# A step's preparation split into two streams, with three expected times set anew, in a planned recurrent layer

## The chip, the cores and the metric

The kernel runs on one core of one Trainium2 chip. The metric is the device time of one execution in microseconds, the median of three runs. TensorE (PE) multiplies, VectorE (DVE) and ScalarE (ACT) do elementwise work and empty PSUM, GpSimd (POOL) helps, and SyncE (SP) issues the DMAs.

## The reference

One layer over 1024 prompt tokens and 8 x 16 sample tokens, model width 1024, 16 heads of 64. In short form:

```python
h = rmsnorm(x, g_norm); proj = h @ w_in            # columns: r k v w_lr a_lr z_a | gb gc xb z_b | g_a g_b
pa = proj_a + mu_shift * (previous_token - proj_a)   # token shift on r, k, v, w_lr, a_lr, z_a
w = exp(-c * sigmoid(w_decay0 + tanh(w_lr) @ w_decay2)); a = sigmoid(w_iclr0 + a_lr @ w_iclr2)
kt = k * (1 + (a - 1) * k_replace); kh = k * k_removal / norm_of_head(k * k_removal)
# for each token: S = S * w - (S kh) (a * kh)^T + v kt^T ;  y = S r
o_a = (group_norm(y) + sum_of_head(r * kt * r_bonus) * v) * silu(z_a)
out_b = (gb * conv3(gc * xb) * silu(z_b)) @ w_o_b
x = x + (sigmoid(g_a) * (o_a @ w_o_a) + sigmoid(g_b) * out_b) @ w_out
x = x + sigmoid(rmsnorm(x, g_ple) @ w_ple_gate) * (p @ w_ple); y = rmsnorm(x, g_final)
```

It also returns the new states. The recurrence is computed in chunks of 64 tokens.

## The kernel before, in words

Every projection is a "dense": 8 steps over the contraction, of three f16 matmuls each (high and low parts), into one of two PSUM banks of the pool `psd`. Tokens come in three blocks: 512 prompt tokens, the 128 sample tokens, 512 prompt tokens. Heads come in 8 pairs. A *step* is one pair and one block, so there are 24 steps; step `i` has pair `j = i // 3` and block `g = i % 3`.

Most of the time is one loop (`go`), in which the order of TensorE's instructions is planned when the program is built. Ten kinds of work are Python generators; a `Stream` runs one kind, one step (or column tile) at a time. The planner keeps a clock of its own, `pe[0]`, which each matmul advances by a cost. A generator yields a number (not before so many us from now), a number and a count of PSUM banks of the pool `psp` that it needs, a condition, or DENSE or MORE (a part of a projection comes next). `go` first takes a stream that isn't a projection and is due, in the order of the list `every`; if there is none it takes a projection part, one begun before a new one. Convolution projections (`conv`) go ahead of the others when they are behind a pace counted in chunks of the recurrence, and behind them otherwise. The order that comes out is TensorE's order on the chip; the other engines' orders are made by the scheduler from the order of the program and priorities.

The streams of a step:

- `prep` (L365): `decay` multiplies the low-rank inputs (`lod`, `loa`) and makes the decay products `pb` and `pi`; then the projections `k`, `r`, `v`, `z` in this order, each mixed with the token before it (`mixed`). After `r`, squares of `k` are summed per head (`pss`, 4.0 us expected) and the inverse norms `rnb` made by a chain of small VectorE operations and one ScalarE copy (L442). Before `v`, the generator waits until the tail of step `i - 3` is through (`S_tail.at >= f.i - 2`; `v` and `zs` have three buffers). After `v`, 3.0 us expected, `rnb` is transposed (`prn`), and `k`, `kt` and `tha` are finished on VectorE. After `z` comes its tanh, then `keys`.
- `keys` (L467) makes the operands `ar` and `kb` of the scores (`kb` has one buffer: it waits for `kb_done` of the step before) and `rkt`.
- `scores` (L497) waits until the step before has read its scores (`m_done`, `x_done`), then, 1.0 us expected, multiplies `kb` and `ar` (`psc`) into two banks. `values` transposes `kb` and `v` (`pk`, `pv`). `inverse` (`itt`, `ig`, `i`, `ie`, `if`) inverts the chunks' triangular matrices. `chain` is the recurrence, three matmuls per chunk (`c`, `u`, `u`), 8 chunks in a prompt step and 2 in a sample step. `tail` makes the output (`y`, `py`).
- `opening` brings in the three blocks at the start, `conv` makes the other branch, and `gates_b` computes up to six merge gates (`EARLY`) into DRAM once the convolution is done and as long as tails are left.

Behind the loop come the remaining gates, the three output projections and the embedding stage; an early gate is loaded from DRAM (`gb_d`) there.

Ring buffers that matter: seven stage buffers (`TA`) for the intermediate tiles of `prep`, and six pairs of projection weights (`whi`, `wlo`), loaded on SP and split by ScalarE and VectorE; the weights of the next pair are loaded when the third block has used those of this pair.

Of the kernel before, what the change touches and what calls it, by code (L numbers as in the profile page):

```python
# [23 lines left out]
RN = 512  # L24
# [47 lines left out]
def _build(nc, tc, I, O, top):  # L72
# [292 lines left out]
    def prep(f):  # L365
# [39 lines left out]
            tha, pb, pt, pi = yield from decay()  # L405

        m = {}
        ahead = g == 2 and j + 1 < 8
        for q, t in (("k", T_K), ("r", T_R), ("v", T_V), ("z", T_ZA)):
            load_q(j, q)  # L410
            if q == "v":
                yield lambda: S_tail.at >= f.i - 2
            ps = yield from dense_parts(s.w[q], blk, q + nm)
            if ahead:
                load_q(j + 1, q)
            if q == "v":
                x = f.v = tt(wk, "v", "v" + nm, 3, RN)[:, :n]
            elif q == "z":
                x = f.zs = tt(wk, "zs", "zs" + nm, 3, RN)[:, :n]
            else:  # L420
                x = tt(st_, "ta", q + nm, TA)[:, :n]
            mu = (zmu[:, i, j:j + 1] for i in range(3)) if q == "z" else (
                P("mu", t + j), mum[:, t + j:t + j + 1], mus[:, t + j:t + j + 1])
            mixed(ps, t + j, blk, x, *mu, q + nm)
            m[q] = x
            if q == "k" and not f.i:
                f.k_done = True
                tha, pb, pt, pi = yield from decay()
            if q == "r":
                x = m["k"]  # L430
                yield 4.0

                sq = tt(st_, "ta", "sq" + nm, TA)[:, :n]
                A.activation(sq, x, AF.Square, scale=P("krem", j))
                pss = psa.tile([128, 512], F32, tag="a", name="pss" + nm)
                for i in range(npr):
                    mm(pss[:, 2 * i:2 * i + 2], sq[:, i * 128:(i + 1) * 128], onesb[:, 0:128:64], start=True, stop=True)
                ssm = small.tile([128, 8], F32, tag="ssm", name="ssm" + nm)
                V.tensor_scalar(out=ssm[:, :2 * npr], in0=pss[:, :2 * npr], scalar1=1e-24, scalar2=None, op0=ALU.max)
                rn = rsqrt(ssm[:, :2 * npr], 2 * npr, "k%d" % npr)  # L440
                rnb = tt(st_, "ta", "rnb" + nm, TA)[:, :n]
                A.activation(rnb.rearrange("p (q t) -> p q t", t=64), rn.unsqueeze(2).to_broadcast([128, 2 * npr, 64]),  # L442
                             AF.Copy)
            if q == "v":

                k = m["k"]
                yield 3.0
                prn = psa.tile([128, 512], F32, tag="a", name="prn" + nm)
                for i in range(npr):
                    tr(prn[:, i * 128:(i + 1) * 128], rnb[:, i * 128:(i + 1) * 128], ident)  # L450
                kt = tt(st_, "ta", "kt" + nm, TA)[:, :n]
                V.tensor_scalar(out=kt, in0=tha, scalar1=half[:, 2, j:j + 1], scalar2=half[:, 3, j:j + 1],
                                op0=ALU.mult, op1=ALU.add)
                V.tensor_tensor(out=kt, in0=kt, in1=k, op=ALU.mult)
                V.scalar_tensor_tensor(out=k, in0=k, scalar=P("krem", j), in1=prn[:, :n], op0=ALU.mult, op1=ALU.mult)
                V.scalar_tensor_tensor(out=tha, in0=tha, scalar=1.0, in1=k, op0=ALU.add, op1=ALU.mult)
        if ahead:
            load_lora(j + 1)
        z = m["z"]

        thz = tt(st_, "ta", "thz" + nm, TA)[:, :n]
        A.activation(thz, z, AF.Tanh)
        V.scalar_tensor_tensor(out=f.zs, in0=thz, scalar=1.0, in1=z, op0=ALU.add, op1=ALU.mult)
        f.pt = pt
        yield from keys(f, m["k"], kt, tha, m["r"], pb, pi)

    def keys(f, kh, kt, b2, r, pb, pi):  # L467
        j = f.j
# [28 lines left out]
    def scores(f):  # L497
# [7 lines left out]
        np2 = min(2, npr)  # L505
        msk = sm_s if smp else sm_p
        for p0 in range(0, npr, 2):
            yield 1.0, 2
            pss = [psp.tile([128, 2, 2, 128], F32, tag="p", name=f"psc{nm}_{p0}{h}")[:, :np2] for h in range(2)]
            for p in range(np2):  # L510
                for e in range(2):
                    for x in range(2):
                        for h, H in enumerate(HS):
                            mm(pss[h][HS[x], p, e, :], kb[H, p0 + p, 2 * e + x, :],
                               ar[H, 2 * (p0 + p) + e].rearrange("p a b -> p (a b)"), start=True, stop=True)
            hold(1.3)
            hold(2.2)
            for h in range(2):
                pf4 = pss[h].rearrange("p c e (x t) -> p c (e x) t", x=2)
                V.tensor_tensor(out=scx[:, h, p0:p0 + np2], in0=pf4[:, :, 1:3, :],  # L520
                                in1=msk[:, 64:128].unsqueeze(1).unsqueeze(1).to_broadcast([128, np2, 2, 64]), op=ALU.mult)
                V.tensor_tensor(out=scy[:, h, p0:p0 + np2], in0=pf4[:, :, 0:4:3, :],
                                in1=msk[:, 0:64].unsqueeze(1).unsqueeze(1).to_broadcast([128, np2, 2, 64]), op=ALU.mult)
# [348 lines left out]
    class Stream:  # L872
# [28 lines left out]
        def fill(self):  # L901
            return self.next in (DENSE, MORE)

    S_chain, S_tail, S_val, S_inv, S_scores, S_open, S_prep, S_conv, S_gate = every = [
        Stream(k) for k in (chain, tail, values, inverse, scores, opening, prep, conv, gates_b)]
    may = {S_chain: lambda i: S_inv.at > i and S_val.at > i and S_tail.at >= i - 1,
           S_tail: lambda i: S_chain.at > i,
           S_val: lambda i: S_scores.at > i and S_chain.at >= i - 1 and (i < 2 or steps[i - 2].y_done),
           S_inv: lambda i: S_scores.at > i,
           S_scores: lambda i: S_prep.at > i and (i < 3 or steps[i - 3].y_done),  # L910
           S_prep: lambda i: S_chain.at >= i - 3 and S_open.at >= (0, 2, 3)[min(i, 2)],
# [31 lines left out]
    rk.close()  # L943


    ow = top.enter_context(tc.tile_pool(name="ow", bufs=1, side="right"))
    mr = top.enter_context(tc.tile_pool(name="mr", bufs=1, side="right"))
    oo = top.enter_context(tc.tile_pool(name="oo", bufs=1))
# [45 lines left out]

    obs = []
    for j in range(KT):
        if T_GB + j not in EARLY:
            gate(ms[j], T_GB + j, f"b{j}")
            for k in range(2 * (j - 4), 2 * (j - 3)):
                obs.append(load_o(ob_d, k, f"b{k}"))  # L1000
    for j in range(KT):
        if T_GB + j in EARLY:
            SP.dma_start(ms[j], gb_d[EARLY.index(T_GB + j)])
        w = load_wr(I["w_ob"][j], f"b{j}")
        for blk in BL3:
            o, n = blk
            ps = dense_r(w, obs, blk, f"ob{j}_{o}")
            V.scalar_tensor_tensor(out=ms[j][:, o:o + n], in0=ms[j][:, o:o + n], scalar=1.0, in1=ps,
                                   op0=ALU.add, op1=ALU.mult)
# [2 lines left out]

    def gate_a(j):
        gts[j] = op.tile([128, NTOK], F32, tag="gt", name=f"gt{j}", bufs=2)
        if T_GA + j in EARLY:
            SP.dma_start(gts[j], gb_d[EARLY.index(T_GA + j)])
        else:
            gate(gts[j], T_GA + j, f"a{j}")

# [242 lines left out]
```

## Time and profile before

| what | value |
|---|---|
| median of 3 runs | 1888.74 us (1888.63 to 1889.81) |
| the profiled execution | 1887.54 us |
| its span, first to last instruction | 1885.7 us |
| TensorE busy | 1795.6 us (95%) |
| VectorE busy | 1250.5 us (66%) |
| ScalarE busy | 815.2 us (43%) |
| granted clock of TensorE, mean | 0.991 |

The profile is of one execution. Busy time counts the union of an engine's instructions; matmuls overlap, and their ends are modelled. Names are the program's tiles: `dk`, `dr`, `dv`, `dz` are the projections of a step, `dC`, `dx`, `dzb`, `dB` those of the convolution, `dgb`, `dga` the gates.

### The profile page before, as it was taken

The numbers are of one execution on the slowest core, as the hardware profiler recorded it, in microseconds if no ns is written. First come the engines' busy times: TensorE is split into PE (matmuls) and PEld (weight loads), VectorE is DVE, ScalarE is ACT, GpSimd is POOL, SyncE is SP. The second block draws the span as 40 slices with busy tenths as digits, with TensorE's granted clock in tenths as the row PEclk, the third lists the DMA queues.
The fourth block names the chain that finished last, engine by engine and source line by source line (L and its number), as shares of the span: only waits on it lengthen the run. The fifth ranks groups of instructions, "written<-read, shape, count | busy, mean of one in ns | idle before, by whom it ended". The sixth has DMA issues, their size and how long they took to land.

```text
span 1885.7 us, 37719 instructions
## 1 busy us (share of the span) xinstructions
PE 1795.6 (95%) x15326; PEld 1242.4 (66%) x15326; DVE 1250.5 (66%) x3181; ACT 815.2 (43%) x1871; POOL 210.8 (11%) x333
## 2 busy tenths in 40 slices
PE   5999999999999999999999999999999999999997
PEld 2555665565666666566566556565499777999865
DVE  5577887788688788788788878861422411545566
ACT  6454463554555446446446446442311311333332
POOL 1001121111112111111101101100000011200000
PEclk9999999999999999999999999999999999999998
DMA  6011102011111101101100200221512410242012
GB/s 223 12 35 49 53 17 76 22 33 54 36 33 48 52 31 42 60 31 36 63 31 24 76 29 16 64 86 64 170 58 65 133 45 23 85 157 91 13 32 79
DMA packets 45198, 110.65 MB, mean 59 GB/s; under 512 B 6368, under 2 KB 21344, under 8 KB 45024
## 3 DMA queue, kind: packets, MB, share of 16 engines
q1 hardware_dynamic: 45024, 108.24, 17.9%
q8 instruction: 120, 1.97, 0.4%
q14 instruction: 54, 0.44, 0.1%
HBM read 87.94 MB, written 20.28 MB: 57 GB/s over the span
## 4 chain that ended last, share of the span: by engine, by line
PE 66%; DVE 20%; ACT 7%; DMA 3%; issue 2%; POOL 1%; SPq 0%; DVEq 0%; ACTq 0%
PE ob L92 5%; PE oc L92 5%; PE oa L92 5%; PE dr L92 4%; PE pg L92 4%; PE dz L92 4%; PE dga L92 4%; PE dgb L92 4%; PE dk L92 3%; PE dB L92 3%; PE dzb L92 3%; PE dv L92 3%; PE u L92 2%; PE dC L92 2%; PE dx L92 2%
## 5 line engine op out<-in xcount | busy, mean ns | idle before, releaser
L92 PEld LDWEIGHTS <-whip 128*128 128x128 f16 x1536 | 132.7, 99 | 72.1 <-issue 6.5
L687 POOL TENSOR_SCALAR Spt<-sbd,pt 128x128 f32<-128x128 f32 x128 | 91.3, 713 | 612.0 <-DVE sbd L706 611.0
L706 DVE SCALAR_TENSOR_TENSOR sbd<-u,pt,Spt 64x64 f32<-64x64 f32 x256 | 72.1, 282 | 68.7 <-PE u L92 65.7
L92 PEld LDWEIGHTS <-wlop 128*128 128x128 f16 x768 | 75.5, 98 | 61.8 <-issue 2.2
L92 PE MATMUL dgb<-hx,whigb 128*128 128x512 f16 (+1 forms) x480 | 110.4, 326 | 3.9 <-ACT ms L993 3.5
L627 ACT ACTIVATE bdgt<-ig 64x512 f16<-64x512 f32 (+1 forms) x208 | 106.5, 512 | 2.7
L92 PE MATMUL dB<-hx,whiB 128*128 128x512 f16 (+1 forms) x384 | 90.5, 331 | 4.4 <-ACT sho L233 4.4
L92 PE MATMUL dx<-hx,whiX 128*128 128x512 f16 (+1 forms) x384 | 90.1, 328 | 2.8 <-ACT sho L240 2.8
L92 PE MATMUL dC<-hx,whiC 128*128 128x512 f16 (+1 forms) x384 | 89.9, 328 | 2.1 <-ACT sho L233 2.1
L92 PE MATMUL dzb<-hx,whiZ 128*128 128x512 f16 (+1 forms) x384 | 88.1, 326 | 3.4 <-ACT sho L233 1.7
L92 PE MATMUL dv<-hx,whip 128*128 128x512 f16 (+1 forms) x384 | 90.1, 329 | 0.9 <-DVE zb L829 0.9
L694 ACT ACTIVATE yst<-c 64x128 f32<-64x128 f32 x144 | 38.9, 270 | 119.4 <-DVE xs L693 117.6
L92 PE MATMUL dz<-hx,whip 128*128 128x512 f16 (+1 forms) x384 | 90.5, 329 | 0.0
L92 PE MATMUL dr<-hx,whip 128*128 128x512 f16 (+1 forms) x384 | 90.0, 329 | 0.0
L92 PE MATMUL dk<-hx,whip 128*128 128x512 f16 (+1 forms) x384 | 88.1, 326 | 0.0
L92 PEld LDWEIGHTS <-pg 128*128 128x128 f16 x768 | 65.7, 99 | 27.7 <-issue 3.2
L620 ACT ACTIVATE gt<-ig 128x512 f16<-128x512 f32 (+1 forms) x104 | 54.2, 521 | 67.1 <-PE ig L92 66.6
L628 DVE CAST_PREDICATED tt<-cph,i 128x512 f16<-128x512 uint16 (+1 forms) x104 | 61.8, 594 | 29.9 <-PE i L92 26.0
L700 ACT ACTIVATE vu<-u 64x64 f32<-64x64 f32 x288 | 62.7, 218 | 39.8 <-PE u L92 36.2
L92 PE MATMUL dgb<-hx,wlogb 128*128 128x512 f16 (+1 forms) x240 | 74.4, 326 | 0.0
L634 DVE CAST_PREDICATED tn<-cph,i 128x512 f16<-128x512 uint16 (+1 forms) x104 | 61.3, 589 | 9.1 <-PE i L92 8.8
L92 PEld LDWEIGHTS u<-xs,tm 128*128 128x128 f32 x288 | 51.7, 192 | 22.6 <-DVE xs L693 5.4
(332 smaller groups left out, 4898.3 us busy)
## 6 DMA issues: line engine op xcount, KB each, us to landing
wstp<-i_w_in SPq DMA_DIRECT2D x32, 512.0 KB, 3.5
wstgb<-i_w_in SPq DMA_DIRECT2D x10, 512.0 KB, 3.5
xt<-i_x SPq DMA_DIRECT2D x9, 512.0 KB, 6.1
ob_d<-zb SPq DMA_DIRECT2D x8, 576.0 KB, 2.9
ostb<-ob_d SPq DMA_DIRECT2D x24, 192.0 KB, 2.6
osta<-oa_d SPq DMA_DIRECT2D x24, 192.0 KB, 2.5
xr<-i_xT SPq DMA_DIRECT2D x8, 576.0 KB, 3.6
wstC<-i_w_in SPq DMA_DIRECT2D x8, 512.0 KB, 3.5
```

The source lines that it names most:

```text
L92: PE.matmul(out, lhsT, rhs, start=start, stop=stop)
L620: A.activation(Gt, pg, AF.Copy, scale=-1.0)
L627: A.activation(Gb[R, :, R], pg[R], AF.Copy, scale=-1.0)
L628: V.copy_predicated(out=Tt, mask=bc(lvt[:, b, :]).bitcast(U16), data=p1)
L634: V.copy_predicated(out=Tn, mask=bc(lv[:, b, :]).bitcast(U16), data=p2)
L687: G.tensor_scalar(out=Spt, in0=S, scalar1=pt[:, c:c + 1], scalar2=None, op0=ALU.mult)
L694: A.activation(yst[Vh, p, :], pc[Vh, 0:128], AF.Copy)
L700: A.activation(vu[Uh, c, H], pu[H, H], AF.Copy, scale=-1.0)
L706: V.scalar_tensor_tensor(out=S2[H, H], in0=pu[H, 128 + h * 64:192 + h * 64], scalar=pt[H, c:c + 1], in1=Spt[H, H], op0=ALU.mult, op1=ALU.add)
```

## The change

`prep` is split. A new stream, `prep_v`, makes `v` and `z` and the gate `zs`; `prep` keeps `decay`, `k`, `r`, the norms and `keys`. The steps that the four projections share become the function `project`. `prep_v` stands before `prep` in the list of streams; its step `i` may start when the tail of step `i - 3` is through, which `prep` no longer waits for, and `values` waits for it. Three numbers change: the transposed norms are expected 8.0 us after the sums (3.0 us after `v` before), the first scores of a step 5.0 us after they may start (1.0 before), and the list of gates that count as early becomes as long as the loop got.

```diff
@@ -405,24 +405,8 @@
             tha, pb, pt, pi = yield from decay()
 
         m = {}
-        ahead = g == 2 and j + 1 < 8
-        for q, t in (("k", T_K), ("r", T_R), ("v", T_V), ("z", T_ZA)):
-            load_q(j, q)
-            if q == "v":
-                yield lambda: S_tail.at >= f.i - 2
-            ps = yield from dense_parts(s.w[q], blk, q + nm)
-            if ahead:
-                load_q(j + 1, q)
-            if q == "v":
-                x = f.v = tt(wk, "v", "v" + nm, 3, RN)[:, :n]
-            elif q == "z":
-                x = f.zs = tt(wk, "zs", "zs" + nm, 3, RN)[:, :n]
-            else:
-                x = tt(st_, "ta", q + nm, TA)[:, :n]
-            mu = (zmu[:, i, j:j + 1] for i in range(3)) if q == "z" else (
-                P("mu", t + j), mum[:, t + j:t + j + 1], mus[:, t + j:t + j + 1])
-            mixed(ps, t + j, blk, x, *mu, q + nm)
-            m[q] = x
+        for q in "kr":
+            x = m[q] = yield from project(f, q)
             if q == "k" and not f.i:
                 f.k_done = True
                 tha, pb, pt, pi = yield from decay()
@@ -441,10 +425,9 @@
                 rnb = tt(st_, "ta", "rnb" + nm, TA)[:, :n]
                 A.activation(rnb.rearrange("p (q t) -> p q t", t=64), rn.unsqueeze(2).to_broadcast([128, 2 * npr, 64]),
                              AF.Copy)
-            if q == "v":
 
                 k = m["k"]
-                yield 3.0
+                yield 8.0
                 prn = psa.tile([128, 512], F32, tag="a", name="prn" + nm)
                 for i in range(npr):
                     tr(prn[:, i * 128:(i + 1) * 128], rnb[:, i * 128:(i + 1) * 128], ident)
@@ -454,15 +437,36 @@
                 V.tensor_tensor(out=kt, in0=kt, in1=k, op=ALU.mult)
                 V.scalar_tensor_tensor(out=k, in0=k, scalar=P("krem", j), in1=prn[:, :n], op0=ALU.mult, op1=ALU.mult)
                 V.scalar_tensor_tensor(out=tha, in0=tha, scalar=1.0, in1=k, op0=ALU.add, op1=ALU.mult)
-        if ahead:
+        if g == 2 and j + 1 < 8:
             load_lora(j + 1)
-        z = m["z"]
-
-        thz = tt(st_, "ta", "thz" + nm, TA)[:, :n]
+        f.pt = pt
+        yield from keys(f, m["k"], kt, tha, m["r"], pb, pi)
+
+    def project(f, q):
+
+        j, nm, blk = f.j, f.nm, f.blk
+        s = pair(j)
+        t = {"k": T_K, "r": T_R, "v": T_V, "z": T_ZA}[q]
+        load_q(j, q)
+        ps = yield from dense_parts(s.w[q], blk, q + nm)
+        if f.g == 2 and j + 1 < 8:
+            load_q(j + 1, q)
+        if q in "vz":
+            x = tt(wk, "v" if q == "v" else "zs", ("v" if q == "v" else "zs") + nm, 3, RN)[:, :blk[1]]
+        else:
+            x = tt(st_, "ta", q + nm, TA)[:, :blk[1]]
+        mu = (zmu[:, i, j:j + 1] for i in range(3)) if q == "z" else (
+            P("mu", t + j), mum[:, t + j:t + j + 1], mus[:, t + j:t + j + 1])
+        mixed(ps, t + j, blk, x, *mu, q + nm)
+        return x
+
+    def prep_v(f):
+
+        f.v = yield from project(f, "v")
+        z = f.zs = yield from project(f, "z")
+        thz = tt(st_, "ta", "thz" + f.nm, TA)[:, :f.blk[1]]
         A.activation(thz, z, AF.Tanh)
         V.scalar_tensor_tensor(out=f.zs, in0=thz, scalar=1.0, in1=z, op0=ALU.add, op1=ALU.mult)
-        f.pt = pt
-        yield from keys(f, m["k"], kt, tha, m["r"], pb, pi)
 
     def keys(f, kh, kt, b2, r, pb, pi):
         j = f.j
@@ -505,7 +509,7 @@
         np2 = min(2, npr)
         msk = sm_s if smp else sm_p
         for p0 in range(0, npr, 2):
-            yield 1.0, 2
+            yield 1.0 if p0 else 5.0, 2
             pss = [psp.tile([128, 2, 2, 128], F32, tag="p", name=f"psc{nm}_{p0}{h}")[:, :np2] for h in range(2)]
             for p in range(np2):
                 for e in range(2):
@@ -901,11 +905,12 @@
         def fill(self):
             return self.next in (DENSE, MORE)
 
-    S_chain, S_tail, S_val, S_inv, S_scores, S_open, S_prep, S_conv, S_gate = every = [
-        Stream(k) for k in (chain, tail, values, inverse, scores, opening, prep, conv, gates_b)]
+    S_chain, S_tail, S_val, S_inv, S_scores, S_open, S_pv, S_prep, S_conv, S_gate = every = [
+        Stream(k) for k in (chain, tail, values, inverse, scores, opening, prep_v, prep, conv, gates_b)]
     may = {S_chain: lambda i: S_inv.at > i and S_val.at > i and S_tail.at >= i - 1,
            S_tail: lambda i: S_chain.at > i,
-           S_val: lambda i: S_scores.at > i and S_chain.at >= i - 1 and (i < 2 or steps[i - 2].y_done),
+           S_pv: lambda i: S_tail.at >= i - 2 and S_open.at >= (1, 2, 3)[min(i, 2)],
+           S_val: lambda i: S_scores.at > i and S_pv.at > i and S_chain.at >= i - 1 and (i < 2 or steps[i - 2].y_done),
            S_inv: lambda i: S_scores.at > i,
            S_scores: lambda i: S_prep.at > i and (i < 3 or steps[i - 3].y_done),
            S_prep: lambda i: S_chain.at >= i - 3 and S_open.at >= (0, 2, 3)[min(i, 2)],
@@ -943,6 +948,8 @@
     rk.close()
 
 
+    early = EARLY[:S_gate.at]
+    assert len(early) >= 4
     ow = top.enter_context(tc.tile_pool(name="ow", bufs=1, side="right"))
     mr = top.enter_context(tc.tile_pool(name="mr", bufs=1, side="right"))
     oo = top.enter_context(tc.tile_pool(name="oo", bufs=1))
@@ -994,13 +1001,13 @@
...
-        if T_GB + j not in EARLY:
+        if T_GB + j not in early:
...
-        if T_GB + j in EARLY:
-            SP.dma_start(ms[j], gb_d[EARLY.index(T_GB + j)])
+        if T_GB + j in early:
+            SP.dma_start(ms[j], gb_d[early.index(T_GB + j)])
...
```

## Rows read from the trace of the kernel before

**Rows 1.** Busy time, share of the span and instructions of two engines, from the page

```profile
PE 1795.6 (95%) x15326; PEld 1242.4 (66%) x15326; DVE 1250.5 (66%) x3181; ACT 815.2 (43%) x1871; POOL 210.8 (11%) x333
```

**Rows 2.** Busy time by stretch: start and end, length, then each engine

```profile
core 0: us, PE busy (x) PEld busy (x) DVE busy (x) ACT busy (x) POOL busy (x), PEclk, DMA share, GB/s
0.00:97.00 97.00, 71.78 (x448) 40.58 (x448) 56.94 (x134) 56.51 (x100) 8.21 (x22) 0.95 0.34 118
...
97.00:1341.00 1244.00, 1197.59 (x11588) 756.15 (x11587) 960.34 (x2555) 616.90 (x1495) 176.13 (x287) 0.99 0.15 46
...
640.00:787.40 147.40, 142.72 (x1419) 91.26 (x1417) 121.69 (x325) 77.09 (x188) 22.02 (x37) 1.00 0.13 43
787.40:934.80 147.40, 142.63 (x1418) 91.16 (x1417) 121.62 (x325) 77.02 (x188) 22.02 (x37) 1.00 0.13 42
1215.00:1341.00 126.00, 122.66 (x1041) 73.24 (x1040) 58.05 (x151) 43.43 (x105) 9.35 (x14) 1.00 0.25 87
```

**Rows 3.** TensorE's waits, 640 to 787 us: total us, times, longest

```profile
PE c L92 <- DVE sbd L706: 0.8, 1, 0.8
PE pk L96 <- DVE scy L522: 0.8, 1, 0.8
...
PE psc L92 <- DVE scy L522: 0.5, 2, 0.3
```

**Rows 4.** TensorE's waits, 97 to 545 us

```profile
PE dB L92 <- ACT sho L233: 4.4, 2, 2.3
PE dx L92 <- ACT sho L240: 2.8, 2, 2.5
PE dC L92 <- ACT sho L233: 2.1, 1, 2.1
```

**Rows 5.** TensorE in order of time, 745 to 833 us: start, length, instruction

```profile
745.47 1.05 PE L92 MATMUL pss<-cpk,sq 128*128 128x2 f32 x8 [0.27 <-ACT vu L551]
...
756.42 0.66 PE L96 MATMUL py<-ident,yc 128*128 128x128 f32 x4 [0.34 <-DVE yc L761]
...
758.43 0.59 PE L92 MATMUL dv<-hx,whip 128*128 128x512 f16 x2 [0.23 <-DVE zb L829]
...
768.55 0.63 PE L96 MATMUL prn<-ident,rnb 128*128 128x128 f32 x4
...
778.20 1.10 PE L92 MATMUL psc<-ar,kb 64*64 64x128 f32 x32
...
809.89 1.03 PE L92 MATMUL pss<-cpk,sq 128*128 128x2 f32 x8
...
815.01 0.45 PE L92 MATMUL y<-vu,scy 128*64 128x64 f32 x8
...
829.86 0.40 PE L92 MATMUL if<-tn,bdgt 128*128 128x64 f16 x8
...
832.69 0.38 PE L92 MATMUL c<-sbd,ar 128*128 128x128 f32 x2
```

**Rows 6.** Busy time in three stretches behind waits and one unbroken gate projection

```profile
316.00:319.30 3.30, 3.30 (x10) 1.29 (x9) 0.00 (x0) 0.00 (x0) 0.00 (x0) 0.50 0.33 130
469.60:472.90 3.30, 3.30 (x12) 2.01 (x11) 1.88 (x4) 0.44 (x2) 0.00 (x0) 0.50 0.17 71
111.20:114.60 3.40, 3.12 (x15) 1.49 (x15) 2.35 (x8) 0.58 (x2) 0.62 (x3) 0.50 0.01 2
1473.00:1484.30 11.30, 11.30 (x72) 5.88 (x72) 5.93 (x10) 5.56 (x11) 0.00 (x0) 1.00 0.52 160
```

**Rows 7.** ScalarE in order of time: the norms of two steps

```profile
757.35 0.63 ACT L442 ACTIVATE rnb<-nrk 128x512 f32<-128x512 f32 x1 [2.75 <-DVE nrk L139]
...
816.37 0.63 ACT L442 ACTIVATE rnb<-nrk 128x512 f32<-128x512 f32 x1 [0.85 <-DVE nrk L139]
```

**Rows 8.** VectorE in order of time: the key products of one step

```profile
762.41 0.68 DVE L489 TENSOR_TENSOR kb<-kt,pi 128x512 f32<-128x512 f32 x1
...
773.57 0.69 DVE L490 SCALAR_TENSOR_TENSOR kb<-tha,pi 128x512 f32<-128x512 f32 x1
```

More of the change, by code (lines that the diff above doesn't have):

```diff
@@ L1014, in gate_a @@
         gts[j] = op.tile([128, NTOK], F32, tag="gt", name=f"gt{j}", bufs=2)
-        if T_GA + j in EARLY:
-            SP.dma_start(gts[j], gb_d[EARLY.index(T_GA + j)])
+        if T_GA + j in early:
+            SP.dma_start(gts[j], gb_d[early.index(T_GA + j)])
         else:
```

## The prediction

> **What bounds the kernel now.** I read the page's busy shares first, then busy time by stretch, then who TensorE waited for, and last the order of events around one step of the third block. TensorE is busy 1795.6 us of a span of 1885.7, VectorE 1250.5 [rows 1]. By stretch, three regimes show [rows 2]: an opening of 97 us with 25.2 us idle, the recurrent loop from 97 to 1341 us with 46.4 us idle in 1244, and a projection stage with hardly any. Inside the loop the picture repeats every 147.4 us, the time of one pair of heads: the two stretches shown hold 142.7 and 142.6 us of TensorE work, so 4.7 and 4.8 us idle. No gap is left that one could close at one place: the steady idle is made of waits of 0.8 us and less [rows 3], while VectorE is busy 121.7 of the 147.4 us. The larger waits all lie before 545 us: projections that wait until ScalarE has emptied a PSUM bank (4.4 + 2.8 + 2.1 us) [rows 4].
>
> The chain of the recurrence does pause. In the pair shown, the short sample chain ends before 815.01 us (its `y`), and the next chain's first matmul stands at 832.69, right after that step's inverse (`if`, 829.86) [rows 5]. That inverse is late because its step is: the sums `pss` come at 745.47, but `v` only at 758.43, after `py` of an older tail at 756.42; then `prn` at 768.55 and the scores at 778.20 [rows 5]. So 17.7 us of pause per pair hang on a wait for a tail that keys don't need. But TensorE doesn't pause there; projections fill it. The reader should hold two facts apart: the chain has slack in it, TensorE has almost none.
>
> The Trainium skill (Perfetto Trace Analysis, Identifying the Most-Contended Engine) says that matmul busy time is a bad measure of distance to the roofline, and that the share of LDWEIGHTS should be used. By it the pair at 640 us (91.3 of 147.4 us, 62%) would leave room, and closing the pause would pay 17.7 us a pair. The trace disagrees: 72 projection matmuls that run without a break fill 11.30 of 11.30 us with only 5.9 us of weight loads (52%) [rows 6], so 62% is no room here.
>
> **The change part by part.** Times are set against the profiled execution, 1887.5 us (span 1885.7 and 1.8 around it); the median of the runs is 1.2 higher, so a difference is added to 1888.7.
>
> *Matmuls, DMAs, operations.* None is added or removed in the loop: the same four projections, sums, transposes and scores per step, and the same weight loads, which stay attached to the projection that they precede (the next pair's `v` and `z` weights are now issued from the value stream). Sum: 0. The list of early gates becomes as long as the loop got; a gate that isn't made in the loop is made later, 11.30 us for 72 matmuls [rows 6] at either place, and its trip through DRAM falls away. That is 0 as long as gates still cover the loop's end; the loop's last stretch is 122.7 of 126 us busy [rows 2], and the four gates behind the loop stay there as cover.
>
> *Keys no longer wait for the tail.* Scores, inverse and chain of the third block can come up to 17.7 us earlier. What hides this is TensorE's own work: 142.7 us a pair must be done anyway, and the convolution is paced by chunks, so a chain that gets ahead calls in convolution work and is slowed again. Value 0. Its bounds: nothing, or at best all idle time of the loop, 46.4 us.
>
> *Transposed norms: 3.0 us after `v` become 8.0 us after the sums.* In the step at 745.47 the norms `rnb` were ready at 757.35 + 0.63, so 12.5 us after the sums began; in the next step 7.1 us (809.89 to 816.37 + 0.63) [rows 5, 7]. Neither cost anything, because `v`'s projection lay between. Now TensorE's queue reaches `prn` 8.0 us after the sums' 0.9 us, so 8.9 us. A step like the second waits 0, one like the first 3.6 us, and behind `prn` the whole queue waits, chain matmuls too. Bounds: 0, or 3.6 in one step of each of 8 pairs, 29 us. I take 4 us, nearer to the cheap row: keys now run earlier against the tail whose VectorE work made that step late.
>
> *Scores: 1.0 becomes 5.0 us.* `z`'s projection stood between `prn` and the scores. In the step shown the last key product ended at 773.57 + 0.69, 5.7 us after `prn` began [rows 5, 8]; the allowance is now 0.5 + 5.0. So 0.2 us a step are missing. But the first key product ended at 762.41 + 0.68, 17.6 us after the sums, and `prn` now comes after 8.9; if VectorE serves it no sooner, scores at 8.9 + 5.5 wait 3.2 us. Bounds 0 and 8 x 3.2 = 26 us; I take 2, since scores also wait for the preceding step's values.
>
> *`v` and `z` back to back.* In the sample step these are short projections. PSUM has two banks for projections, and the trace shows the price of two short ones in a row: `dx` waits 2.5 us for a bank, and behind that wait the granted clock is 0.5, the 1.2 GHz level, from 111.2 to 114.6 us [rows 4, 6], which costs up to 1.7 us more. Bounds: 0, because chain and inverse matmuls between them cover it (the steady pairs show no such wait), or 4.2 us in each of 8 pairs, 34 us. I take one such event, 4 us.
>
> *Waits that dissolve.* The order of projections is drawn anew, so the three kinds of bank waits before 545 us (9.3 us) and the slow clock behind three of them (3 x 1.7) [rows 6] need not recur; steady pairs live without them. Bounds 0 and -14.4; I take -12, all but one.
>
> The wait for the tail moves to a stream on which only projections `v` and `z` are queued; `values` waits for it, and needs it only after the previous chain. 0, and covered by convolution work; if that were used up, the pause above would come back, at 17.7 us a pair.
>
> *Moved along.* The next pair's low-rank weights (four small DMAs on SP, one ScalarE and one VectorE operation) are issued ahead of `v` and `z` instead of behind; they are needed a step later, so 0. The tanh of `z` takes one of seven stage buffers that the keys also use; if none is free, ScalarE's queue stands until the norms are transposed. The nearest row is its 2.75 us of idle time before `rnb` [rows 7]; bounds 0 and 2.8 us in each of 8 pairs, 22 us. I take 0, because ScalarE is busy only 77 of 147.4 us [rows 2].
>
> At the start, `v` and `z` of step 0 now precede `r`, and its scores wait 4 us longer; other projections cover both, 0, and at most 4 us.
>
> Sum: 4 + 2 + 4 - 12 = -2 us, so **1886.7 us**.
>
> **Rivals.** *A: norms late (slower).* VectorE is busy 82% of a pair [rows 2]; if the sums of one step per pair still fall beside a tail, `prn` blocks the queue. Seven pairs at 3.6 us instead of my 4 in all: 1886.7 + 21 = 1908, and 1920 if the slow clock follows each. It decides from norms later than 8.9 us. For it speaks the 12.5 us, against it the 7.1. *B: short projections collide (slower).* 4.2 us in every other pair gives 1886.7 + 13 = 1900, in every pair 1917. *C: the loop loosens (faster).* With keys ready ahead of need, scores and inverse no longer crowd the same microseconds; the 14.4 us go and half of the steady 4.7 us in the last five pairs, 12 us: 1888.7 - 26 = 1862 at best, and half of it 1876. *D: TensorE has room (faster).* Then seven pauses close, 7 x 17.7 = 124: 1765 us. The 4.7 us of idle a pair speak against it. The page of the Trainium skill named above would have it so. *E: it doesn't do what it says.* The scores could be held by something else than their keys; then order and waits stay, 1888.7. For it speaks that scores wait for their PSUM banks, too (0.5 us a pair) [rows 3]; against it that those of the third block start 9.6 us behind `prn`, once `z` is through [rows 5].
>
> **How the numbers follow.** A measurement can tell about 0.2%, 3.8 us. My forecast, work kept and small waits traded, has 0.35, with a range of its own of 1880 to 1895: 0.13 faster, 0.18 the same, 0.04 slower. A has 0.17 and B 0.12, all slower. C has 0.20 and D 0.03, all faster. E has 0.13: 0.09 the same, 0.02 and 0.02 to either side. Sums: faster 0.38, same 0.27, slower 0.35. From 1870 to 1908 little is left out: D, the best part of C and the worst parts of A and B.
>
> **What would show it.** TensorE's loop work stays 142.7 us a pair; the waits column then decides. `prn <- rnb` at zero clears A, a row of 20 us or more proves it. `dz`, `dk` or conv projections waiting for ScalarE prove B. Scores of the third block should follow their sums by some 15 us instead of 32.7, and the pause of 17.7 us should shrink while the pair's 147.4 us do not. If the pair shortens below 143 us, my reading of TensorE as full is wrong.

## The result, and the profile after

The change makes the kernel slower: 1933.83 us (1933.39 to 1937.75, 4 runs) against 1888.68 us (4 runs of before on the same chip), a ratio of 1.0248 [1.0232, 1.0264]. The forecast was 1886.7, with a range up to 1908.

The page's busy shares and the windows of the kernel after, to be read beside [rows 1, 2]:

```profile
PE 1796.6 (93%) x15326; PEld 1244.0 (64%) x15326; DVE 1249.6 (65%) x3181; ACT 815.9 (42%) x1871; POOL 227.1 (12%) x333
```

```profile
0.00:97.00 97.00, 71.41 (x459) 40.23 (x460) 54.53 (x132) 54.61 (x99) 8.98 (x22) 0.96 0.35 120
97.00:1387.00 1290.00, 1199.08 (x11579) 758.33 (x11577) 963.54 (x2560) 620.45 (x1497) 190.58 (x287) 0.99 0.14 45
1387.00:1931.60 544.60, 526.09 (x3291) 445.43 (x3290) 231.57 (x492) 140.88 (x276) 27.56 (x24) 0.99 0.24 75
```

TensorE does the same work (1796.6 us against 1795.6), and so does the loop (1199.1 against 1197.6). The loop ends 46 us later, and its idle time is 1290 - 1199.1 = 90.9 us where it was 46.4: 44.5 us more, the whole loss. The opening and the stage behind the loop keep theirs (25.6 and 18.5 us now).

TensorE's waits in this loop, the largest rows, and two small ones on which the forecast rested (total us, times, longest):

```profile
PE py L96 <- DVE yc L765: 9.0, 5, 3.7
PE psc L92 <- DVE bdgt L651: 8.1, 3, 4.1
PE py L96 <- ACT vu L555: 5.7, 3, 2.4
PE dk L92 <- ACT sho L240: 5.6, 3, 2.6
PE dC L92 <- ACT sho L240: 5.0, 3, 2.5
PE lod L92 <- ACT vu L555: 5.0, 9, 1.5
PE dx L92 <- ACT sho L233: 4.9, 2, 3.3
PE dC L92 <- ACT cs L793: 3.4, 4, 1.5
...
PE prn L96 <- ACT rnb L426: 2.7, 2, 1.6
PE dr L92 <- ACT sho L233: 2.6, 1, 2.6
```

No row dominates; there are many waits of one to four microseconds, most of them for a PSUM bank. The largest row is not: `py` transposes `yc`, and waits until VectorE has scaled it (L765). The view that gives idle time by group of instructions allows a sum by the PSUM pool that the waiting matmul writes into:

| pool: tiles | before, 97 to 1341 us | after, 97 to 1387 us |
|---|---|---|
| `psd`: projections (`dB`, `dx`, `dzb`, `dC`, `dv`, `dk`, `dr`, `dgb`) | 4.4 + 2.8 + 3.4 + 2.1 + 0.9 + 0 + 0 + 0.4 = 14.0 | 2.3 + 6.6 + 3.9 + 8.4 + 0.4 + 10.2 + 7.2 + 0 = 39.0 |
| `psa`: small tiles (`py`, `lod`, `prn`, `psb`, `pss`, `y`) | 5.7 + 0 + 0 + 1.9 + 1.1 + 0 = 8.7 | 15.2 + 5.6 + 3.3 + 0.7 + 0.3 + 0.3 = 25.4 |
| `psp`: scores, values, inverse | 14.8 | 20.5 |
| `psc`: the chain (`c`, `u`, `pS`) | 4.9 + 3.1 + 0 = 8.0 | 1.1 + 4.3 + 0.3 = 5.7 |

So +25.0 for projections, +16.7 for small tiles, +5.7 for scores and what follows them, -2.3 for the chain; with 0.8 less before the first output projection, and rounding, that is the 44.5. Not all of it is waiting for a bank: of the small tiles' 25.4 us, 9.0 are `py` waiting for `yc` and 2.7 `prn` waiting for the norms `rnb` (5.7 and 0 before).

One of these waits in TensorE's order of time, with ScalarE beside it:

```profile
1025.59 0.38 PE L92 MATMUL lod<-lrd,lwh 128*128 128x512 f16 x1 [1.53 <-ACT vu L555]
...
1026.02 0.27 PE L92 MATMUL dv<-hx,whip 128*128 128x128 f16 x2
...
1029.76 0.28 PE L92 MATMUL dz<-hx,whip 128*128 128x128 f16 x2
...
1031.55 0.22 PE L92 MATMUL dz<-hx,wlop 128*128 128x128 f16 x1
1034.38 0.59 PE L92 MATMUL dk<-hx,whip 128*128 128x512 f16 x2 [2.61 <-ACT sho L240]
```

```profile
1032.08 0.62 ACT L397 ACTIVATE pb<-cum 128x512 f32<-128x512 f32 x1
1032.60 0.62 ACT L401 ACTIVATE pi<-cum 128x512 f32<-128x512 f32 x1
1033.23 0.37 ACT L226 ACTIVATE v<-dv,mum 128x128 f32<-128x128 f32 x1
...
1034.15 0.18 ACT L240 ACTIVATE sho<-dv 128x8 f32<-128x8 f32 x1 [0.29 <-DVE v L238]
```

`dv` and `dz` of the sample block are short and now stand back to back. `dz` is done in 2.0 us, and the next key projection needs the bank that `dv` left. ScalarE is busy with other work, the decay products `pb` and `pi` last, reads `dv` at 1033.23, 3.5 us after its last matmul began (1029.70), and the bank is free after the copy of the last tokens at 1034.15. Behind `dk` all of TensorE's queue stands for 2.61 us.

### The profile page after: what moved, and what is told of

The parts are those of the page before. It is cut to its first block, busy times and chain, and to the rows that moved or that the text cites. A ratio compares the mean times of both kernels' runs of the same rounds, so it can differ in the third digit from the quotient of the medians.

```text
span 1931.6 us, 37755 instructions
## 1 busy us (share of the span) xinstructions
PE 1796.6 (93%) x15326; PEld 1244.0 (64%) x15326; DVE 1249.6 (65%) x3181; ACT 815.9 (42%) x1871; POOL 227.1 (12%) x333
## 4 chain that ended last, share of the span: by engine, by line
PE 65%; DVE 22%; ACT 6%; issue 3%; DMA 3%; POOL 0%; POOLq 0%; SPq 0%; DVEq 0%; ACTq 0%
PE ob L92 5%; PE oc L92 5%; PE oa L92 5%; PE dgb L92 4%; PE pg L92 4%; PE dr L92 4%; PE dC L92 4%; PE dga L92 4%; PE dv L92 3%; PE dk L92 3%; PE dzb L92 3%; PE dz L92 3%; PE dx L92 3%; PE dB L92 2%; PE u L92 2%
## 5 line engine op out<-in xcount | busy, mean ns | idle before, releaser
L92 PE MATMUL dk<-hx,whip 128*128 128x512 f16 (+1 forms) x384 | 88.7, 326 | 10.2 <-ACT sho L240 5.6
L92 PE MATMUL dzb<-hx,whiZ 128*128 128x512 f16 (+1 forms) x384 | 88.8, 326 | 3.9 <-ACT sho L233 3.3
L92 PE MATMUL dz<-hx,whip 128*128 128x512 f16 (+1 forms) x384 | 89.2, 327 | 0.0
L632 DVE CAST_PREDICATED tt<-cph,i 128x512 f16<-128x512 uint16 (+1 forms) x104 | 61.8, 595 | 20.3 <-PE i L92 18.5
L697 DVE TENSOR_TENSOR xs<-c,vu 64x128 f32<-64x128 f32 x144 | 41.3, 287 | 43.7 <-PE c L92 41.2
```

The lines of the kernel that those rows point to most:

```text
L92: PE.matmul(out, lhsT, rhs, start=start, stop=stop)
L632: V.copy_predicated(out=Tt, mask=bc(lvt[:, b, :]).bitcast(U16), data=p1)
L697: V.tensor_tensor(out=xs[Uh, :], in0=pc[Uh, 0:128], in1=vu[Uh, c, :], op=ALU.add)
```

## The experiments

The view and stretch named with a number are those of the run in question; the kernel before beside each run gave 1887.7 to 1889.3 us.

**One part undone, one part alone.** First the scores: the new 5.0 taken back, and the 5.0 alone in the kernel before.

```
e1 (after):   yield 1.0 if p0 else 5.0, 2   ->  yield 1.0, 2
e2 (before):  yield 1.0, 2                  ->  yield 1.0 if p0 else 5.0, 2
```

> The changed kernel with the first scores of a step expected 1.0 us after they may start, as before, instead of 5.0. If the longer time for the scores were the cause (it counts anew after the wait for the preceding step, and shifts every step), the time should fall from 1934 to about 1890 to 1900 us. If the cause is where the projections and the keys stand, it stays within 10 us of 1934, and the waits of the scores grow by a few us, because the keys are not ready after 1.0 us.

Measured: 1971.9 us, 1.0441 [1.0411, 1.0472]. The row that grew is the scores' wait for their keys, so the 5.0 does in the new order what it is meant to, and is worth 38 us there:

```profile
PE psc L92 <- DVE ar L489: 15.8, 6, 4.5
```

Only half of the 38 us is waiting: TensorE's busy time for the same matmuls also grew, by 20.0 us to 1816.6, at a mean granted clock of 0.979 instead of 0.990.

> The kernel before with one number changed: the first scores of a step expected 5.0 us after they may start, instead of 1.0. If the longer time alone shifts the pattern to a worse one, the time rises by 10 us or more. If it costs nothing where keys are ready (the theory that the order of projections is the cause), it stays between 1885 and 1893 us.

Measured: 1934.44 us, 1.0240 [1.0210, 1.0270]. One number, without any split, costs the old order as much as the whole change. Its loop idles 82.0 us (1288 - 1205.99), 41.0 of them ahead of projections. So the split isn't needed for the loss, and the parts don't add up: each is good or bad in the order that the others make.

Then the place of the value stream (exchanged with `prep` in `every`), and the wait for the tail given back to the norms:

```
e3 (after):  S_open, S_pv, S_prep, S_conv  ->  S_open, S_prep, S_pv, S_conv      (and the kinds with them)
e4 (after):  yield 8.0                     ->  yield 8.0; yield lambda: S_tail.at >= f.i - 2
```

> The changed kernel with the key stream ahead of the value stream in the planner's list. If v and z that push in ahead of k and r, back to back, are the cause, the time falls by more than half of the 45 us, to below 1911. If it is that keys, values and tail of neighbouring steps fall together, nothing of that changes and the time stays within 10 us of 1934.

Measured: 1907.39 us, 1.0100 [1.0071, 1.0129]. With `k` and `r` ahead of `v` and `z`, 26.4 of the 45 us are gone; projections wait 23.9 us in the loop instead of 39.0. The exchange draws the whole order anew, so it doesn't price these places alone.

> The changed kernel, but the transposed norms, and with them the keys, again wait until the tail of step i-3 is through, as v did before. If freeing the keys from the tail bunches the work of ScalarE and VectorE, the 45 us come back to a large part: 1890 to 1905. If the split into two streams itself costs (v and z late or back to back), the time stays above 1920.

Measured: 1934.14 us, 1.0241 [1.0212, 1.0271]. That keys no longer wait for the tail costs nothing and brings nothing on the whole.

**Mending the banks from the planner's side.** In e5 the instructions that empty a projection's bank got a high priority on ScalarE and VectorE, TensorE's order kept. In e7 (on after) and e8b (on before) the planner counts two projection banks, each busy for 3.5 us after its projection, and starts none before; e8b also counts as early only the gates that the loop made, as the change does.

```
e5 (after), in mixed:   with first():   # tc.high_priority(offset=4000) around its instructions
e7, e8b, in go:         fills = more or (dense if min(dbank) <= pe[0] else [])
                        dbank[dbank.index(min(dbank))] = pe[0] + 3.5      # when a projection is done
```

> The changed kernel, with the operations that empty a projection's bank for k, r, v, z (the mixing) at high priority in ScalarE's and VectorE's order. TensorE's order stays the same. The waits of projections for a bank are 39.0 us in the loop, 14.1 before. If late emptying is the price, they fall to about 15 us and the time by about 25 us, to 1910. If ScalarE and VectorE are simply full at those places, the wait goes elsewhere (py, psc, u) and the time stays within 8 us of 1934.

Measured: 1925.9 us, 1.0198 [1.0168, 1.0227]. The projections' waits fall from 39.0 to 25.1 us, but ScalarE's and VectorE's other work now comes later; the chain's waits grow from 5.7 to 8.6.

> The changed kernel with a planner that knows the two banks of the projections: a projection may start only when one of them was left at least 3.5 us ago on the planner's clock. If TensorE's waits for those banks (39.0 us in the loop) come from projections queued too close behind each other, with other work due meanwhile, they fall below 15 us and the time falls by 15 to 25 us, to about 1910 to 1919. If nothing else is due at these places, the waits only move and the time stays within 8 us of 1934.

Measured: 1945.14 us, 1.0296 [1.0267, 1.0326].

> The kernel before with the same planner that knows the projections' banks (and the list of early gates cut to those made). Its bank waits are 14.1 us in the loop. If the rule is good in itself, the time falls to 1876 to 1886; if the order before is good by its own pattern and any other order loses it, the time rises above 1893.

Measured: 1922.64 us, 1.0177 [1.0148, 1.0207]. The rule that should save waits costs the old order 33 us and the new one 11. In the new order it does save some (26.4 us ahead of projections instead of 39.0); in the old one it doesn't (`dz` alone waits 13.2 us, and waited for nothing before). The orders that it draws also wait elsewhere: in e7 13.0 us ahead of `psc`, in e8b 8.5 us in `c` for `sbd`. But e7 isn't slower by its waits: its idle time in the span falls from 135.0 us (1931.6 - 1796.6) to 128.3 (1941.7 - 1813.4). What grows, by 16.8 us, is the busy time of the same matmuls, at a mean granted clock of 0.984 instead of 0.990:

```profile
PE 1813.4 (93%) x15326; PEld 1252.2 (64%) x15326; DVE 1248.4 (64%) x3181; ACT 814.9 (42%) x1871; POOL 230.5 (12%) x333
```

**The last token's copy on VectorE** (the kernel before):

```
A.activation(sho.., ps[:, n - 1:n], AF.Copy, scale=IWS)  ->  V.tensor_scalar(out=sho.., in0=ps[:, n - 1:n], scalar1=IWS, ...)
```

> The kernel before, with the copy of a projection's last token moved from ScalarE to VectorE, behind VectorE's reading of the same bank (the order on TensorE stays). ScalarE stood idle 64 us in the loop before these copies, waiting for VectorE. If that hold-up makes the banks come free late, the bank waits fall by half and the time by 5 to 10 us, to 1879 to 1884. If not, the time is within 4 us of 1888.6, or VectorE's 72 operations more cost some us.

Measured: 1883.48 us, 0.9973 [0.9958, 0.9989]. It is faster, but not by its waits. Before 545 us they are those of [rows 4] under another name:

```profile
PE dB L92 <- DVE sho L233: 4.3, 2, 2.3
PE dx L92 <- DVE sho L240: 2.8, 2, 2.4
```

The copy is only the last of the readers; the bank waits for the mixing ahead of it. What fell is TensorE's busy time (1791.4 us instead of 1795.6), at a mean clock of 0.994 instead of 0.991; why the clock was higher is not shown.

**Is any new order bad?** By now it looked as if the order before were a lucky draw. Two unrelated numbers of the kernel before were moved by half a microsecond, and the scores by half of the way.

```
e13: tail, yield 11.0 -> 11.5      e14: sums, yield 4.0 -> 4.5      e12: scores, 1.0 -> 3.0
```

> The kernel before with one number of another stream moved by half a microsecond: the tail of a step is expected after 11.5 instead of 11.0 us. Theory 'the order before is a favourable one': half a microsecond is enough to draw the loop's order anew, and a new order loses 15 to 55 us to many small waits for banks, as those of the scores' 5.0 did: 1904 to 1944. Rival 'the later scores have a price of their own': a shift that has nothing to do with scores costs nothing, 1881 to 1897.

> The kernel before with the sums of squares expected after 4.5 instead of 4.0 us, all else as it was. Theory 'the order before is a favourable one': 1904 to 1944. Rival 'the later scores have a price of their own': 1881 to 1897.

> The kernel before with the first scores of a step expected after 3.0 instead of 1.0 us, half of the step to 5.0, which cost 45 us by itself. Rival 'the later scores have a price of their own': the price grows with the delay, so about half of it, 1905 to 1918. Theory 'the order before is a favourable one': no proportion; a new order loses anything from 15 to 55 us, 1904 to 1944, and one at or above 1925 would speak against a price that grows with the delay.

Measured: 1884.18 (0.9984 [0.9973, 0.9996]), 1886.63 (0.9996 [0.9982, 1.0009]) and 1930.93 us (1.0225 [1.0208, 1.0241]). The lucky draw falls in the form that was put on record: half a microsecond doesn't draw the order anew. Both controls change the order from the first pair on, and cost nothing, but they change it little. Counted in the traces, 99% of TensorE's matmuls stand within 20 places of where they stood; in e11 below it is 32%, in the kernel after 30%. So the controls don't show that a really different order could be as good, and every run with one took longer than the kernel before, 1899 to 1972 us. The price by the delay fares no better: 3.0 costs nearly what 5.0 does. What parts the runs shows in one stretch, 545 to 1200 us. First the windows of the kernel before and of e13:

```profile
545.00:1200.00 655.00, 632.27 (x6307) 405.74 (x6305) 539.38 (x1442) 345.98 (x842) 100.32 (x169) 1.00 0.13 41
```

```profile
545.00:1200.00 655.00, 631.96 (x6285) 405.62 (x6280) 540.83 (x1447) 344.90 (x841) 102.25 (x166) 1.00 0.13 42
```

Then the only row of projections among TensorE's waits there, in before and in e13:

```profile
PE dv L92 <- DVE zb L829: 0.9, 4, 0.2
```

```profile
PE dv L92 <- DVE zb L829: 1.6, 4, 0.4
```

Both run in a rhythm in which projections hardly wait: 0.9 and 1.6 us in 655. The controls keep the same pairs. Before 545 us the kernel before pays as others do (4.4 + 2.8 + 2.1 us in [rows 4]). So the good order survives small shifts: it is a rhythm, and half a microsecond doesn't leave it.

**Where the rhythm is lost.** The scores at 2.0:

> The kernel before with the scores expected after 2.0 us instead of 1.0 (3.0 cost 43 us, 5.0 cost 45). Theory 'the loop either falls into the repeating order or not': nothing between, 1881 to 1893 with pairs that repeat in 147 us and waits for projections of under 3 us between 545 and 1200 us, or 1920 to 1940 with some 20 us of them there. Rival 'a price by the delay': 1905 to 1915.

Measured: 1919.5 us, 1.0170 [1.0155, 1.0185], just under the one theory's range and above the rival's. The same stretch, its largest row (4.6 us before), and the largest of its 14 waits of projections (17.8 us together; after has 21.4 there):

```profile
545.00:1200.00 655.00, 617.64 (x5983) 391.14 (x5984) 503.47 (x1334) 316.42 (x772) 96.44 (x155) 0.98 0.13 41
```

```profile
PE py L96 <- DVE yc L761: 12.0, 3, 5.4
PE dzb L92 <- ACT sho L233: 6.7, 4, 2.4
PE dx L92 <- ACT sho L233: 6.2, 3, 2.9
PE dC L92 <- ACT cs L789: 1.8, 2, 1.3
```

The loop to 1375 idles 1278 - 1208.2 = 69.8 us, 23.4 more than before. Over the whole span the loss of 31 us is 25.9 us more idle time (1916.8 - 1800.8 = 116.0 instead of 90.1) and 5.2 us more busy time for the same matmuls:

```profile
PE 1800.8 (94%) x15326; PEld 1243.3 (65%) x15326; DVE 1251.3 (65%) x3181; ACT 812.4 (42%) x1871; POOL 216.6 (11%) x333
```

Behind some of these waits the granted clock drops, as in [rows 6]. This run, at the end of the 2.9 us wait:

```profile
938.50:941.80 3.30, 2.71 (x7) 1.22 (x7) 1.76 (x5) 0.57 (x2) 0.78 (x2) 0.50 0.47 150
```

The place can be read off. Around the scores of the first block of a pair, the kernel before and then e11:

```profile
689.69 0.28 PE L92 MATMUL dx<-hx,whiX 128*128 128x128 f16 x2
...
690.90 1.10 PE L92 MATMUL psc<-ar,kb 64*64 64x128 f32 x32
691.93 0.49 PE L92 MATMUL c<-sbd,ar 128*128 128x128 f32 x2
...
692.82 0.22 PE L92 MATMUL dx<-hx,wloX 128*128 128x128 f16 x1
692.87 0.28 PE L92 MATMUL dk<-hx,whip 128*128 128x128 f16 x2
```

```profile
649.43 0.28 PE L92 MATMUL dx<-hx,whiX 128*128 128x128 f16 x2
...
650.72 0.22 PE L92 MATMUL dx<-hx,wloX 128*128 128x128 f16 x1
652.38 0.59 PE L92 MATMUL dx<-hx,whiX 128*128 128x512 f16 x2 [1.44 <-ACT sho L233]
...
653.33 1.10 PE L92 MATMUL psc<-ar,kb 64*64 64x128 f32 x32
```

What holds the bank in e11 is the gate projection ahead of them, which ended at 648.95; its last reader on ScalarE:

```profile
652.15 0.17 ACT L233 ACTIVATE sho<-dz 128x1 f32<-128x1 f32 x1 [1.62 <-DVE zs L231]
```

In both kernels a short `dx` follows `dz`, whose bank takes 3.4 us to empty in e11 (648.95 to 652.32). At 1.0 us the first scores are due while the short `dx` runs; with a chain matmul and `loa` they stretch it to 3.2 us, and `dk` finds its bank free. At 2.0 us `dx` is through in 1.5 us before the scores are due, the next projection is begun, and waits 1.44 us. The test: scores at 2.0, but due 1.0 sooner while a short projection runs.

```
e21 (before, scores 2.0), in go:  soon = 1.0 if cur[0] == 128 and any(x.next == MORE for x in live) else 0.0
                                  # S_scores counts as due at ready - soon
```

> The kernel before with the scores expected after 2.0 us (1919.5), but due 1.0 us sooner, so after the old 1.0 us, while a projection of the 128-token block is running: the first scores can then stand inside the short projection behind a gate projection and stretch it while the gate's bank is emptied. Theory 'the scores no longer cover the bank that the gate projection left': the time goes back to 1881 to 1897. Rival 'the place of the scores matters through the whole rhythm, not through this one cover': 1908 to 1925.

Measured: 1899.04 us, 1.0055 [1.0041, 1.0069], between the two ranges. The cover gives back 20 of the 31 us, and the projections' waits in the loop fall from 36.6 to 18.4 us. What stays above all is the wait of the tail's transposes for VectorE; `py` waits 13.0 us in the loop of e11 and 16.9 here:

```profile
PE py L96 <- DVE yc L764: 16.9, 5, 6.3
```

So scores that stretch a short projection are the larger part of what the step from 1.0 to 2.0 costs. The edit makes scores due sooner inside every short projection, so it doesn't single out this one place; what the rest is, isn't shown.

**Are the bank waits the loss, or do they only move?** TensorE's order stays the same instruction for instruction, but the bank is read once, by ScalarE; the mixing and the copy of the last token read the result in SBUF. The kernel so leaves out the shift by one token, while the work of each engine stays of the same size:

```
V.scalar_tensor_tensor(out=out[:, 1:n], in0=ps[:, 0:n - 1], ...)   ->  in0=t1[:, 1:n]      (SBUF)
A.activation(sho[:, ct, 0:1], ps[:, n - 1:n], ...)                 ->  out[:, n - 1:n]     (SBUF)
```

> The kernel after, TensorE's order the same instruction for instruction, but the bank of a key, receptance, value or gate projection is read once, by ScalarE; VectorE's mixing and the copy of the last token read the copy in SBUF instead (the shift by one token is left out, so the values are not the reference's; the work of each engine stays of the same size). Theory 'banks of the projections': the waits for them (some 39 us of TensorE's idle time in the loop) fall to 10 to 18 us and the time with them, to 1905 to 1917. Rival 'a wait that goes comes back at the next tile': the idle time moves on to the small tiles and scores, and the time stays above 1922, as with the mixing at high priority (1925.9).

> The same edit on the kernel before, its TensorE order kept. Theory 'banks of the projections': it has only 14 us of such waits in the loop, nearly all before 545 us, so it gains 5 to 9 us: 1879 to 1885, and the kernel after in this form is 20 to 35 us behind it instead of 45. Rival 'the projections' banks are not what tells the two orders apart': both kernels gain alike, and 45 us stay between them.

> The same edit on the kernel before with the scores expected after 5.0 us (1934.4 without the edit, with 41 us of waits for the projections' banks). Theory 'banks of the projections': 1903 to 1917. Rival 'a wait that goes comes back at the next tile': above 1922.

Measured: 1912.14 us on after (1.0138 [1.0120, 1.0156]), 1875.79 on before (0.9940 [0.9923, 0.9956]), 1906.31 on before with 5.0 (1.0097 [1.0080, 1.0114]). They gain 21.7, 11.9 and 28.1 us; before gains 3 us more than expected, so 36.3 us stay between the two kernels, just over the 20 to 35 foreseen. On after, waits don't move on. In its loop the projections' idle time falls from 39.0 to 16.6 us, about what the time gains, and the other rows are nearly as they were:

```profile
PE py L96 <- DVE yc L765: 8.5, 5, 3.6
PE psc L92 <- DVE bdgt L651: 8.1, 3, 4.1
PE py L96 <- ACT vu L555: 5.7, 3, 2.4
PE lod L92 <- ACT vu L555: 4.1, 8, 1.3
```

In the other two orders a part moves on: projections wait 11.0 us less in e18 and 30.4 less in e19, the span idles 7.6 and 24.3 less. And of the 45 us between the two kernels quick banks take only 9 away. Of the 36.3 left, 13.6 are projections that still wait (16.6 against 3.0 us) and 15.2 the small tiles (24.4 against 9.2).

**Better versions.** The exchange e3 with the copy on VectorE, and the two small gains on the kernel before together:

> The kernel after with keys and receptance ahead of value and gate, as in the run with the two streams exchanged (1907.4), and with the copy of the last token made by VectorE as in the run on the kernel before (1883.5). If the copy's place on ScalarE holds the projections' banks in this order too, the waits for it go from the banks of the projections (27.7 us there) and it gives back 5 to 15 us: 1892 to 1902. If the emptying is bound by ScalarE's and VectorE's other work in whatever order, it gives nothing: 1904 to 1911.

Measured: 1913.19 us, 1.0133 [1.0117, 1.0150]: no gain.

> The kernel before with two things that each gave a little alone: the copy of the last token on VectorE (ratio 0.9973) and the tail expected after 11.5 us (0.9984). If both take time from different waits, the ratio is 0.994 to 0.997; if both only shorten the same waits before 545 us, 0.997 to 0.999.

Measured: 1882.99 us, 0.9966 [0.9954, 0.9978]. It is faster than both kernels; the interval overlaps with e9's, so that the two gains add isn't shown. Neither gain is one of waits: in e9, e13 and e20 the span idles 88.8, 90.0 and 89.2 us (before 90.1), and the busy time falls from 1795.6 us to 1791.4, 1792.6 and 1792.0, at mean clocks of 0.994, 0.993 and 0.994 (0.991).

## Why the prediction was wrong

*TensorE is full: right.* The loop's work moved by 1.5 us. The scores of the step [rows 5] follow their sums by 17.0 us instead of 32.7 (15 expected):

```profile
775.57 0.95 PE L92 MATMUL pss<-cpk,sq 128*128 128x2 f32 x8
...
785.77 0.60 PE L96 MATMUL prn<-ident,rnb 128*128 128x128 f32 x4
...
792.59 0.43 PE L92 MATMUL psc<-ar,kb 64*64 64x128 f32 x2
794.89 1.10 PE L92 MATMUL psc<-ar,kb 64*64 64x128 f32 x30 [1.87 <-DVE bdgt L651]
```

No time came from it, and e4 shows the same from the other side: the term of 0 for the tail was right. The pause of the chain, which should have shrunk, became irregular: gaps of over 6 us between `c` and `u` matmuls sum to 182 us (192 before), and two are over 40. Rival E falls with it, and so do C and D, for the loop idles more, not less. One of the Trainium skill's measures of TensorE's room (Perfetto Trace Analysis, Identifying the Most-Contended Engine), the busy share of weight loads, gives the loop 758.3 of 1290 us, 59%, against 61% before. Here the share fell because idle time was added, and showed no room that could be used.

*Norms, +4, and the list of gates, 0: right.* `prn` waits 3.3 us in the whole loop. Rival A is out; no run undid the 8.0 alone. The list changed nothing, for the loop made all six early gates in both kernels.

*Scores, +2: mis-sized.* `psc` waits 10.1 us where it waited 3.9, and 8.1 of that not for keys but for a bank that `bdgt` of an inverse still holds (the last row above). Keys are in time at 5.0; at 1.0 they are not (e1).

*`v` and `z` back to back, +4, and the waits that dissolve, -12: this is the step that failed.* I took -8 for the projections' banks; the loop paid +25.0. The -12 read "steady pairs live without them" as a property of the kernel. It is one of a rhythm, in which, at the place read above, scores and chain matmuls happen to stretch a short projection; the change gave the rhythm up, and the stretch from 545 to 1200 us pays 21.4 us where it paid 0.9. That these waits are real time is shown (e17: 21.7 us back with TensorE's order kept). That exchanging the two streams takes back over half of the loss is shown, too (e3), but not that it does so by these waits alone. Rival B named the mechanism, with 0.12, but priced only the sample block's own pairs, up to 1917 us.

*Not in the sum at all: small tiles, +16.7.* `lod` of the next step now comes right behind `pv` and `psb` of a step, whose banks ScalarE and VectorE still read (nine waits, 5.0 us); `py` waits for such a bank, too (5.7 us), and for its operand `yc` from VectorE (9.0). The reading of the steady idle as waits of 0.8 us and less, with all larger ones before 545 us, had missed that row. In the kernel before, between 545 and 1200 us:

```profile
PE py L96 <- DVE yc L761: 4.6, 8, 2.0
```

No run undid these alone, so what a mended order would give back there stays open.

*Open as well:* why a number of the scores decides over the whole rhythm, beyond what e21 gave back, and whether any really different order can do without these waits.

## What to carry to other kernels

When one engine is full and its order is planned, look at who empties its banks and not only at the chain that a change of the order frees: here waits for banks were the larger part of the price, and the freed chain brought nothing. For each tile of a ring of two, compare the work that stands between its predecessor's end and its own start with the emptying time. This is a way of reading; as a rule of the planner, with one time for every bank, it lost (e7, e8b). A steady pattern without waits is a property of that pattern; don't take it as a bound for another order, and expect that a number which moves one item by a microsecond can cost 31 us, as in e11, or nothing. Test such numbers one at a time in the old order too, since here the new order needed the 5.0 and the old one lost 45 us by it.

## What was not expected of the hardware

Taking two of the three readers from a projection's bank, with the same work on ScalarE and VectorE, was worth 11.9 us even in the kernel before, whose projections wait 14.0 us in the loop: 3.0 us stay. And the same matmuls didn't always take the same time: 1791.4 us busy in e9 and 1816.6 in e1, at mean granted clocks of 0.994 and 0.979. A wait can cost twice, as in e11, where the clock is 0.50 for 3.3 us at the end of a wait of 2.9 us and the busy time grew by 5.2 us. But it needn't: the kernel after idles 45 us more than before, and its busy time grew by 1.0 us.
